# Storing the last four output tiles of an RMSNorm-matmul in smaller pieces

## The chip, the cores and the metric

One core of a Trainium2 chip. The metric is the device time of one execution in microseconds. Times are medians over several runs, and a kernel is compared with the kernel before by runs of the same rounds on the same chip. The profile covers one execution; its span, from first to last instruction, is some 2 us shorter than the time. The runs below used several chips, and the table of profiles mixes them.

## The reference

```python
def setup_inputs():
    batch, seq, dim, out_dim = 16, 1024, 512, 768
    # x: float32 (batch, seq, dim); gamma: ones; weight: float32 (dim, out_dim) * 0.1; eps = 1e-5

def reference(x, gamma, weight, eps):
    rms = np.sqrt(np.mean(x ** 2, axis=-1, keepdims=True) + eps)
    x_norm = x / rms * gamma
    return np.matmul(x_norm, weight).astype(np.float32)
```

That is 16,384 rows. The kernel works on 128 tiles of 128 rows; a tile's output is 128 x 768 float32, 384 KB, 3 KB for each of 128 partitions.

## The kernel before

The kernel casts x to bf16, transposes it on TensorE, multiplies by the weights (gamma folded in), and applies the row's 1/rms when the sums leave PSUM. Outputs gather in groups of eight tiles. A table says after which tile how many tiles are stored at once:

```python
    opening = [1, 2, 1, 2, 2]
    last = NT // OG - 1                       # NT = 128 tiles, OG = 8 tiles in a group
    o_first, o_size = stretches(OG, {0: opening, 1: [4, 4], last - 1: [4, 4], last: [2, 2, 2, 1, 1]})
    ...
    def store(i):
        first, n = o_first[i], o_size[i]
        if i == first + n - 1:
            nc.sync.dma_start(out=rows(out, first, n), in_=held(o_tiles, OG, first, n))
    ...
    def finish_tile(i, acc, engine):
        scale(engine, out_tile(i), acc[:, :O], rstd_of[i])
        store(i)
    ... # the main loop calls finish_tile for all tiles but the last two
        for i in (NT - 2, NT - 1):
            for lo, hi, engine in ((0, WIDE, nc.scalar), (WIDE, O, nc.vector)):   # WIDE = 512, O = 768
                a = accumulator()
                for k in range(K):
                    matmul(i, k, a, lo, hi)
                scale(engine, out_tile(i)[:, lo:hi], a[:, lo:hi], rstd_of[i])
            store(i)
```

Every load of x and every store goes through the sync queue, the queue that the sync engine (SP in the profiles) feeds. Its transfers are spread over 16 DMA engines, each of which moves its share in packets. The last four tiles are called A, B, C and D below (tiles 124 to 127): before, A and B are stored together, C alone, D alone.

Of the kernel before, what the change touches and what calls it, by code (L numbers as in the profile page):

```python
# [18 lines left out]
def kernel(  # L19
# [8 lines left out]
    nc = tc.nc  # L28
# [3 lines left out]
    out = out.flatten_outer_dims()  # L32
# [3 lines left out]
    NT = N // P  # L36
    NP = NT // 2
    XG, OG = 16, 8
# [7 lines left out]
    def stretches(group, parts):  # L46
        first, size, i = {}, {}, 0
        for g in range(NT // group):
            for n in parts.get(g, [group]):
                for t in range(i, i + n):  # L50
                    first[t], size[t] = i, n
                i += n
        return first, size

    opening = [1, 2, 1, 2, 2]
    last = NT // OG - 1
    x_first, x_size = stretches(XG, {0: opening + [4, 4], 1: [4, 4, 8]})
    o_first, o_size = stretches(OG, {0: opening, 1: [4, 4], last - 1: [4, 4], last: [2, 2, 2, 1, 1]})

    def rows(ap, i, n):  # L60
        if i < XG:
            return ap[i * P:(i + n) * P, :].rearrange("(p t) d -> p t d", t=n)
        return ap.rearrange("(g p t) d -> g p t d", p=P, t=XG)[i // XG, :, i % XG:i % XG + n, :]
# [13 lines left out]
    def held(tiles, group, i, n=1):  # L77
        return tiles[i // group][:, i % group:i % group + n, :]
# [8 lines left out]
    def load_until(i):  # L87
        while starts and starts[0] < i:
            load(starts.pop(0))

    def cast(i, engine, n=1):
        if i // 2 not in xb_tiles:
            xb_tiles[i // 2] = xbp.tile([P, 2, D], BF16, name="xb")
        engine.tensor_copy(out=xb_tiles[i // 2][:, i % 2:i % 2 + n, :], in_=held(x_tiles, XG, i, n))  # L94

    def square(i, ssq):
        jk = junk.tile([P, D], BF16, name="jk")
        nc.scalar.activation(out=jk, in_=held(x_tiles, XG, i)[:, 0, :], func=AF.Square, accum_out=ssq)  # L98

    def root(i, n, ssq):  # L100
        rms = stats.tile([P, 4], F32, name="rms")
        nc.scalar.activation(out=rms[:, :n], in_=ssq[:, :n], func=AF.Sqrt, scale=1.0 / D, bias=eps_sb)  # L102
        rstd = stats.tile([P, 4], F32, name="rstd")
        nc.vector.reciprocal(out=rstd[:, :n], in_=rms[:, :n])  # L104
        for t in range(n):
            rstd_of[i + t] = rstd[:, t:t + 1]

    def norms(i, n):
        ssq = stats.tile([P, 4], F32, name="ssq")
        for t in range(n):  # L110
            square(i + t, ssq[:, t:t + 1])
        root(i, n, ssq)
# [18 lines left out]
    def transpose_tile(i):  # L131
        for h in range(2):
            transpose_word(i // 2, i % 2, h)
        evac(i // 2, i % 2, 1)

    def scale(engine, dst, src, r):
        if engine is nc.scalar:
            nc.scalar.mul(out=dst, in_=src, mul=r)  # L138
        else:
            nc.vector.tensor_single_scalar(out=dst, in_=src, scalar=r, op=mybir.AluOpType.mult)  # L140

    def accumulator():
        return opsum.tile([P, 2, WIDE], F32, name="ops").rearrange("p a b -> p (a b)")

    def out_tile(i):
        if i // OG not in o_tiles:
            o_tiles[i // OG] = outp.tile([P, OG, O], F32, name="ot")
        return o_tiles[i // OG][:, i % OG, :]
# [5 lines that stand above are left out]
# [6 lines left out]
    def matmuls(i, acc, ks, feed=None):  # L160
        for k in ks:
            matmul(i, k, acc, 0, WIDE)
            if feed:
                feed()
            matmul(i, k, acc, WIDE, O)
# [4 lines that stand above are left out]
# [16 lines left out]
    with tc.manual_schedule():  # L186
        g_row = singles.tile([2, P, 2], F32)
        nc.scalar.dma_start(out=g_row, in_=gamma.rearrange("(h w c) -> h w c", w=P, c=2))

        wv = weight.rearrange("(h w c) o -> w h (c o)", w=P, c=2)  # L190
        touched = singles.tile([P, 2, 1], F32)
        nc.scalar.dma_start(out=touched, in_=wv[:, :, 0:1])
        nc.scalar.preload_act_table(AF.Sqrt)  # L193
        load_until(3)
        w_f32 = singles.tile([P, K, O], F32)
        for h in range(2):
            nc.sync.dma_start(out=w_f32[:, 2 * h:2 * h + 2, :].rearrange("p c o -> p (c o)"), in_=wv[:, h, :])
        load_until(2 * XG)


        warm = singles.tile([P, WIDE], BF16)
        nc.vector.memset(warm, 0.0)  # L202
        eps_sb = singles.tile([P, 1], F32)
        nc.vector.memset(eps_sb, float(eps))  # L204
        ident_f = singles.tile([P, P], F32)
        make_identity(nc, ident_f)
        spare = accumulator()

        def warm_up(n):
            for _ in range(n):  # L210
                nc.tensor.matmul(out=spare[:, :WIDE], lhsT=warm[:, :P], rhs=warm, start=True, stop=True)  # L211

        w_bf = singles.tile([P, K, O], BF16)

        def weights(k, engine, lo=0, hi=O):
            scale(engine, w_bf[:, k, lo:hi], w_f32[:, k, lo:hi], g_sb[:, k % 2, k // 2:k // 2 + 1])


        ssq = stats.tile([P, 4], F32, name="ssq")
        warm_up(6)  # L220
        cast(0, nc.vector)
        square(0, ssq[:, 0:1])
        gp = tpsum.tile([P, 2, 2], F32, name="tp")
        for c in range(2):
            nc.tensor.transpose(out=gp[:, c, :], in_=g_row[:, :, c], identity=ident_f[:2, :2])  # L225
        g_sb = singles.tile([P, 2, 2], F32)
        nc.vector.tensor_copy(out=g_sb, in_=gp)  # L227
        transpose_tile(0)
        warm_up(3)
        cast(1, nc.vector)  # L230
        cast(2, nc.gpsimd)
        square(1, ssq[:, 1:2])
        square(2, ssq[:, 2:3])
        transpose_tile(1)
        transpose_tile(2)
        warm_up(2)

        acc = [accumulator() for _ in range(4)]
        weights(0, nc.vector, 0, WIDE)
        weights(0, nc.vector, WIDE, O)  # L240
        weights(1, nc.scalar)
        for k in (0, 1):
            for i in range(3):
                matmuls(i, acc[i], [k])
        root(0, 3, ssq)
        weights(2, nc.vector)
        weights(3, nc.scalar)
        cast(3, nc.gpsimd)
        matmuls(0, acc[0], [2, 3])
        finish_tile(0, acc[0], nc.scalar)  # L250
        transpose_tile(3)
        norms(3, 1)
        matmuls(1, acc[1], [2, 3])
        finish_tile(1, acc[1], nc.vector)
        cast(4, nc.gpsimd)
        cast(5, nc.gpsimd)
        matmuls(2, acc[2], [2, 3])
        finish_tile(2, acc[2], nc.scalar)
        matmuls(3, acc[3], [0, 1, 2, 3], feeder([2], [0, 2, 2, 0], alone=True))
        finish_tile(3, acc[3], nc.vector)  # L260
        cast(6, nc.gpsimd, 2)
        cast(8, nc.gpsimd, 2)
        norms(4, 2)


        one, two, both = [1, 1, 0, 1, 1, 0, 0, 0], [1, 0, 1, 0, 1, 0, 1, 0], [1, 1, 1, 1, 1, 1, 1, 1]
        for j in range(2, NP):
            load_until(2 * j + AHEAD)
            if j + 3 < NP:
                cast(2 * j + 6, nc.gpsimd, 2)  # L270
            if j + 1 < NP:
                norms(2 * j + 2, 2)
            if j == NP - 1:
                break
            if j < 4:
                feed = feeder([j + 1], one)
            elif j == 4:
                feed = feeder([5, 6], both)
            elif j + 2 < NP:
                feed = feeder([j + 2], two)  # L280
            else:
                feed = None
            for i, engine in ((2 * j, nc.scalar), (2 * j + 1, nc.vector)):
                a = accumulator()
                matmuls(i, a, range(K), feed)
                finish_tile(i, a, engine)


        for i in (NT - 2, NT - 1):
            for lo, hi, engine in ((0, WIDE, nc.scalar), (WIDE, O, nc.vector)):  # L290
                a = accumulator()
                for k in range(K):
                    matmul(i, k, a, lo, hi)
                scale(engine, out_tile(i)[:, lo:hi], a[:, lo:hi], rstd_of[i])
            store(i)


# [33 lines left out]
```

## Time and profile before

| | before |
|---|---|
| median time | 210.76 us of the first three runs (210.81 with the runs beside the changed kernel) |
| span of the profiled execution | 208.6 us, clock 0.998 |
| PE busy | 95% |
| DMA queue q1, share of 16 engines | 97.0% |
| end of the last scaling | 203.59 us |

The page gives shares over the whole span, then slices of it, then the chain of work that ended last. The last five microseconds show in a table of stretches, which one asks for with chosen limits; after the stretch and its length come the busy times of PE, PEld, DVE, ACT and POOL (TensorE, its weight load, VectorE, ScalarE, GpSimd), and its last columns are the granted clock, the mean busy share of the 16 DMA engines, and GB/s. The prediction shows these lines. A share of 0.06 there is one engine in sixteen. A packet counts in the stretch in which it starts, so a share can come out a little over 1.

### The profile page before, as it was taken

The page shows a single profiled execution, that of the slowest core. Times are in us where ns is not written, and L with a number is a line of the kernel's source. Part 1 is how long each engine was busy: PE and PEld are TensorE (multiplying, and loading weights), DVE is VectorE, ACT ScalarE, POOL GpSimd, SP SyncE. Part 2 cuts the span into 40 slices and gives each one's busy share as a digit, 9 for nine tenths or more (in the row PEclk, how much of TensorE's full clock was granted, in tenths as well). Part 3 has the DMA queues.
Part 4 walks back from the last instruction along what each step waited for, and adds up shares of the span by engine and source line. Part 5 has one row for each costly group of instructions (what it writes and reads, how often), then busy time and mean ns, then how long its engine had stood idle before and what let it go on. Part 6 is the DMA issues. An engine that isn't in the chain of part 4 may idle for free.

```text
span 208.6 us, 3553 instructions
## 1 busy us (share of the span) xinstructions
PE 199.0 (95%) x1268; PEld 137.7 (66%) x1293; DVE 111.6 (54%) x204; ACT 158.2 (76%) x388; POOL 65.8 (32%) x71
## 2 busy tenths in 40 slices
PE   7799999999999999999999999999999999999990
PEld 3366777666766776677667666766776667667650
DVE  2555654654564465456546545654664565456450
ACT  4589787787778778777877877787787778778850
POOL 1058532303631343215323063311533054230000
PEclk9999999999999999999999999999999999999999
DMA  6999999999999999999999999999999999899885
GB/s 216 399 431 415 424 398 433 478 408 394 438 448 421 410 438 434 440 412 424 448 437 432 396 438 438 434 412 432 438 427 456 405 424 437 353 443 386 361 349 225
DMA packets 6630, 85.69 MB, mean 411 GB/s; under 512 B 978, under 2 KB 980, under 8 KB 3156
## 3 DMA queue, kind: packets, MB, share of 16 engines
q1 hardware_dynamic: 6336, 85.46, 97.0%
q8 instruction: 10, 0.16, 0.3%
q10 hardware_dynamic: 276, 0.00, 0.1%
q14 instruction: 8, 0.07, 0.1%
HBM read 35.13 MB, written 50.33 MB: 410 GB/s over the span
## 4 chain that ended last, share of the span: by engine, by line
PE 91%; DMA 3%; DVE 1%; ACT 1%; issue 1%; SPq 0%; DVEq 0%
PE ops L156 78%; PE tp L121 13%; DMA w_f<-in_weight_dram 3%; DVE ot L140 1%; ACT ot L138 0%; SPq L83 0%; ACT jk L98 0%; DVE w_bf L140 0%; DVE xT L128 0%; ACT rms L102 0%; DVE rstd L104 0%; DVEq L140 0%
## 5 line engine op out<-in xcount | busy, mean ns | idle before, releaser
L156 PE MATMUL ops<-w_bf,xT 128*128 128x512 bf16 (+1 forms) x999 | 192.5, 324 | 2.8 <-DVE w_bf L140 1.4
L156 PEld LDWEIGHTS <-xT 128*128 128x128 bf16 x1024 | 100.2, 98 | 57.8 <-issue 1.9
L94 POOL CAST xb<-xt 128x1024 bf16<-128x1024 f32 (+1 forms) x65 | 65.1, 1016 | 120.0 <-PE tp L121 62.2
L128 DVE COPY xT<-tp 128x1024 bf16<-128x1024 bf16 (+1 forms) x67 | 44.5, 667 | 81.0 <-PE tp L121 81.0
L138 ACT ACTIVATE ot<-ops,rstd 128x768 f32<-128x768 f32 (+1 forms) x65 | 58.1, 895 | 37.6 <-PE ops L156 36.8
L98 ACT ACTIVATE jk<-xt 128x512 bf16<-128x512 f32 x128 | 78.7, 619 | 1.1 <-DMA xt<-in_x_dram 1.1
L121 PE MATMUL tp<-ident_f,xb 128*128 128x128 f32 x256 | 69.2, 275 | 0.1
L140 DVE TENSOR_SCALAR ot<-ops,rstd 128x768 f32<-128x768 f32 (+1 forms) x65 | 64.5, 992 | 2.9 <-PE ops L156 2.8
L121 PEld LDWEIGHTS tp<-ident_f,xb 128*128 128x128 f32 x256 | 36.1, 142 | 3.8 <-issue 0.7
L98 ACT ACTIVATION_READ_ACCUMULATOR jk<-xt 128x1 f32 x128 | 24.4, 191 | 0.0
L102 ACT ACTIVATE rms<-ssq,eps_sb 128x2 f32<-128x2 f32 (+1 forms) x64 | 18.9, 296 | 2.0
L104 DVE RECIPROCAL rstd<-rms 128x2 f32<-128x2 f32 (+1 forms) x64 | 10.0, 156 | 3.3 <-ACT rms L102 3.2
L211 PE MATMUL ops<-warm 128*128 128x512 bf16 x11 | 4.8, 585 | 1.2 <-DVE eps_sb L204 1.2
L138 ACT ACTIVATE w_bf<-w_f,g_sb 128x768 bf16<-128x768 f32 x2 | 1.9, 936 | 2.6 <-DMA w_f<-in_weight_dram 2.6
L211 PEld LDWEIGHTS <-warm 128*128 128x128 bf16 x11 | 1.4, 134 | 2.6 <-issue 1.4
L193 ACT ACT_TABLE_LOAD x1 | 1.3, 1283 | 1.8 <-issue 1.8
L94 DVE CAST xb<-xt 128x512 bf16<-128x512 f32 x2 | 1.0, 491 | 2.4 <-DMA xt<-in_x_dram 2.4
L140 DVE TENSOR_SCALAR w_bf<-w_f,g_sb 128x512 bf16<-128x512 f32 (+2 forms) x3 | 1.4, 484 | 1.2 <-DMA w_f<-in_weight_dram 1.2
L225 PEld LDWEIGHTS tp<-ident_f,g_row 2*128 2x128 f32 x2 | 0.3, 201 | 0.8 <-issue 0.8
L202 DVE MEMSET warm<- 128x256 uint32 x1 | 0.3, 272 | 0.9 <-PEq L312 0.9
L225 PE MATMUL tp<-ident_f,g_row 2*128 2x2 f32 x2 | 0.4, 264 | 0.0
L227 DVE COPY g_sb<-tp 128x4 f32<-128x4 f32 x1 | 0.2, 161 | 0.4 <-PE tp L225 0.4
(7 smaller groups left out, 1.0 us busy)
## 6 DMA issues: line engine op xcount, KB each, us to landing
out_dram<-ot SPq DMA_DIRECT2D x12, 3072.0 KB, 15.1
xt<-in_x_dram SPq DMA_DIRECT2D x6, 4096.0 KB, 19.2
out_dram<-ot SPq DMA_DIRECT2D x4, 1536.0 KB, 10.8
out_dram<-ot SPq DMA_DIRECT2D x6, 768.0 KB, 9.6
xt<-in_x_dram SPq DMA_DIRECT2D x4, 1024.0 KB, 13.9
xt<-in_x_dram SPq DMA_DIRECT2D x1, 2048.0 KB, 18.8
xt<-in_x_dram SPq DMA_DIRECT2D x3, 512.0 KB, 6.2
w_f<-in_weight_dram SPq DMA_DIRECT2D x2, 768.0 KB, 7.1
```

The source lines that it names most:

```text
L94: engine.tensor_copy(out=xb_tiles[i // 2][:, i % 2:i % 2 + n, :], in_=held(x_tiles, XG, i, n))
L98: nc.scalar.activation(out=jk, in_=held(x_tiles, XG, i)[:, 0, :], func=AF.Square, accum_out=ssq)
L102: nc.scalar.activation(out=rms[:, :n], in_=ssq[:, :n], func=AF.Sqrt, scale=1.0 / D, bias=eps_sb)
L104: nc.vector.reciprocal(out=rstd[:, :n], in_=rms[:, :n])
L121: nc.tensor.transpose(out=tp_tiles[j][:, t, h, :], in_=words[:, lo:lo + P], identity=ident_f)
L128: nc.vector.tensor_copy(out=dst[:, t:t + n, :], in_=src[:, t:t + n, :])
L138: nc.scalar.mul(out=dst, in_=src, mul=r)
L140: nc.vector.tensor_single_scalar(out=dst, in_=src, scalar=r, op=mybir.AluOpType.mult)
L156: nc.tensor.matmul(out=acc[:, lo:hi], lhsT=xT_tiles[i // 2][:, i % 2, k // 2, :, k % 2], rhs=w_bf[:, k, lo:hi], start=(k == 0), stop=(k == ...
L193: nc.scalar.preload_act_table(AF.Sqrt)
L211: nc.tensor.matmul(out=spare[:, :WIDE], lhsT=warm[:, :P], rhs=warm, start=True, stop=True)
L225: nc.tensor.transpose(out=gp[:, c, :], in_=g_row[:, :, c], identity=ident_f[:2, :2])
```

## The change

Its intent is to start the last stores earlier and to make the very last one small, so that less is left to move after the last scaling.

```diff
-    o_first, o_size = stretches(OG, {..., last: [2, 2, 2, 1, 1]})
+    o_first, o_size = stretches(OG, {..., last: [2, 2, 1, 1, 1, 1]})
@@
                 scale(engine, out_tile(i)[:, lo:hi], a[:, lo:hi], rstd_of[i])
-            store(i)
+                if i == NT - 1:
+                    nc.sync.dma_start(out=rows(out, i, 1)[:, 0, lo:hi], in_=out_tile(i)[:, lo:hi])
+            if i < NT - 1:
+                store(i)
```

(The first two lines are cut; the entries left out are equal.) A and B are stored one by one, and D in two blocks of 512 and 256 columns.

More of the change, by code (lines that the diff above doesn't have):

```diff
@@ L57 @@
     x_first, x_size = stretches(XG, {0: opening + [4, 4], 1: [4, 4, 8]})
-    o_first, o_size = stretches(OG, {0: opening, 1: [4, 4], last - 1: [4, 4], last: [2, 2, 2, 1, 1]})
+    o_first, o_size = stretches(OG, {0: opening, 1: [4, 4], last - 1: [4, 4], last: [2, 2, 1, 1, 1, 1]})
     def rows(ap, i, n):
```

## The prediction

> **What bounds the kernel now.** I read the page first: the busy shares, the slices and the chain that ended last.
>
> ```profile
> PE 199.0 (95%) x1268; PEld 137.7 (66%) x1293; DVE 111.6 (54%) x204; ACT 158.2 (76%) x388; POOL 65.8 (32%) x71
> PEclk9999999999999999999999999999999999999999
> DMA  6999999999999999999999999999999999899885
> ...
> q1 hardware_dynamic: 6336, 85.46, 97.0%
> q8 instruction: 10, 0.16, 0.3%
> ...
> q14 instruction: 8, 0.07, 0.1%
> ...
> PE 91%; DMA 3%; DVE 1%; ACT 1%; issue 1%; SPq 0%; DVEq 0%
> ```
>
> TensorE is the body's bound (91% of the chain, full clock), with the DMA engines hardly less full (97%). The change touches none of the body: the instruction order of PE, DVE, ACT and POOL is the same in both kernels, and only the sync queue gains two issues. So the case is decided in the last microseconds, and I read the timeline of the end next.
>
> ```profile
> 199.17 4.82 SPq L153 DMA_DIRECT2D out_dram<-ot  x4
> 199.20 0.90 ACT L138 ACTIVATE ot<-ops,rstd 128x768 f32<-128x768 f32 x1 [0.37 <-PE ops L156]
> 200.50 1.02 DVE L140 TENSOR_SCALAR ot<-ops,rstd 128x768 f32<-128x768 f32 x1 [1.35 <-PE ops L156]
> 201.37 0.69 ACT L138 ACTIVATE ot<-ops,rstd 128x512 f32<-128x512 f32 x1 [1.26 <-PE ops L156]
> 201.80 0.48 DVE L140 TENSOR_SCALAR ot<-ops,rstd 128x256 f32<-128x256 f32 x1 [0.28 <-PE ops L156]
> 202.67 0.69 ACT L138 ACTIVATE ot<-ops,rstd 128x512 f32<-128x512 f32 x1 [0.61 <-PE ops L156]
> 203.10 0.48 DVE L140 TENSOR_SCALAR ot<-ops,rstd 128x256 f32<-128x256 f32 x1 [0.81 <-PE ops L156]
> ```
>
> Call the last four tiles A, B, C, D. A is scaled by ScalarE until 200.10, B by VectorE until 201.52, C in two blocks until 202.28, D in two blocks until 203.36 (512 columns) and 203.58 (256 columns). Narrow windows of the same view give the stores: the pair before A at 199.17, the pair A+B at 201.60, C at 202.74, D at 203.66. Compute is over at 203.58 and the span at 208.6: 5.0 us of tail. Where they go is in the table of stretches.
>
> ```profile
> 202.00:202.45 0.45, 0.45 (x3) 0.20 (x2) 0.29 (x1) 0.06 (x1) 0.00 (x0) 1.00 0.37 150
> 202.45:204.40 1.95, 0.62 (x5) 0.29 (x3) 0.48 (x1) 0.69 (x1) 0.00 (x0) 1.00 0.98 400
> 204.40:206.40 2.00, 0.00 (x0) 0.00 (x0) 0.00 (x0) 0.00 (x0) 0.00 (x0) 1.00 0.96 382
> 206.40:207.20 0.80, 0.00 (x0) 0.00 (x0) 0.00 (x0) 0.00 (x0) 0.00 (x0) 1.00 0.06 23
> 207.20:208.60 1.40, 0.00 (x0) 0.00 (x0) 0.00 (x0) 0.00 (x0) 0.00 (x0) 0.72 0.00 0
> ```
>
> The last two columns are the DMA engines' mean busy share and GB/s. From 202.45 to 206.40 the engines work off a backlog at 0.96 to 0.98. Before it lies a hole of 0.45 us with a share of 0.37. After it come 0.8 us at 0.06, which is 1/16: one engine alone still has packets. The individual packets say the same: most engines end near 206.42, and then 3 KB packets follow each other about 117 ns apart until 207.18. I call that engine the late one.
>
> Why is it late? The packet lists of two short windows, 193 to 194 and 204.6 to 205.1, show instruction fetches among the data:
>
> ```profile
> q8 instruction: 1, 0.02, 6.3%
> ```
> ```profile
> q14 instruction: 1, 0.01, 3.9%
> ```
>
> The 16 KB fetch of queue 8 starts at 193.45 and takes 1.01 us; a 12 KB data packet beside it takes 1.43 us where the others take 0.46 to 0.50. From there one engine is late. It ends the pair before A at 202.67, when the others ended near 201.98: 0.69 late. It ends A+B at 204.71 (others 204.40): it used the hole to catch up, and was never idle itself. At 204.71, on the heels of that very packet, the 8 KB fetch of queue 14 takes 0.31 us, and that engine's next packets are slower (one takes 294 ns for 121). So it ends 0.75 late.
>
> **What the Trainium skill says.** "DMA: Bandwidth & Descriptors", section "Why a DMA increments its semaphore by 16 and not by 1": a DMA runs on up to 16 engines that finish independently, and only the full count means that all has landed. The trace agrees: of the 16 increments of D's store, 15 are in by 206.87 and the last comes at 207.64. The same page, "Queues, rings and completion order": each engine takes turns between the queue rows that it has work for, by packet; the 1.43 us packet beside the fetch agrees. "Runtime: NRT & Kernel Launch", section "Instruction fetch mechanics": each sequencer fetches its next 16 KiB through DMA; the ten 16 KB fetches of queue 8 are such. The first page's "Anatomy of one DMA" puts most of a fixed cost of some 2 us in the write receipt. Here the last data packet ended at 207.18 and the increment came at 207.64: 0.46 us, less than the page would make one think.
>
> **The change part by part.**
> 1. A is stored alone, so its issue moves from 201.60 (with B) to about 200.18 (A's end 200.10, plus the 0.08 us that lies between B's end and the old issue). An issue reaches the engines 0.85 us later (201.60 to 202.45), so A is ready at 201.03, before the engines end the previous pair at 201.98. The hole of 0.45 us goes, for the 15 engines that have it.
> 2. D in two blocks: the 512 columns issue at 203.36 + 0.08 = 203.44, not 203.66. The 256 columns follow after D's end, 203.66, or after the sync queue is free (0.44 to 0.48 us between back-to-back issues at the start of the kernel): about 203.9. They reach the engines at about 204.75, when there is still over 1 us of backlog. Neither the earlier nor the later one moves the end.
> 3. More packets. Of one store each engine has 8. A 6 KB packet takes 234 ns and a 3 KB packet 121, so a packet costs about 8 ns over its bytes: A+B split is 8 x (2 x 121 - 234) = 64 ns more. For D, 3 KB at 121 becomes 2 KB at 83 (81 to 84 measured for the x loads) and 1 KB at about 46 by the same line: 8 x 8 = 64 ns more. Two more completion writes are 2 x 9 = 18 ns. Sum: +0.15 us per engine.
> 4. The end: the sync engine's records show it passing five semaphore waits in order, and D's completion is in the third of them (207.66); two more at 207.73 and 207.79 and a drain at 207.85 come after it. Completion semaphores go round eight lanes, so the last store moves from the lane of the third wait to that of the fifth. Two waits of 0.063 us no longer lie behind it: -0.13 us.
>
> For 15 engines: -0.45 + 0.15 = -0.30 us. They would end near 206.1. For the late engine: no hole to fill, its bytes and its two fetches are the same, so +0.15 us, at 207.33. The end waits for it. Sum on the path: +0.15 - 0.13 = +0.02 us. The tail keeps its length: 210.76 + 0.02 = 210.78, from which I take a little for the first rival: 210.7.
>
> **The rivals.**
> First, the late engine is less late than the one profile shows. The fetch at 204.71 comes after the last issue, and two more sync instructions could move it or put it on an engine at another moment. Without its 0.31 + 0.17 us the late engine would end at 206.85 and the kernel would gain about 0.45, to 210.3. For it: fetches are not data and nothing fixes their time. Against it: the fetch of queue 8 at 193.45 comes from a long instruction stream that the change leaves alone, and both fetches met the same engine. One in five.
> Second, the drain is not the bound but the last issue's latency: issue to landing is 4.0 us for D. If that were a fixed cost, the later second issue (203.66 to 203.9) would give 211.0. Against it: the share of 0.96 before 206.40 says the 4.0 us are queueing; 0.85 + 0.98 + 0.46 would be 2.3 for a store on idle engines. One in ten.
> Third, 1 KB packets cost as much as 2 KB ones (81 ns): 8 x 35 = 0.28 us more, to 211.0. No 1 KB packets of this queue are in the trace but two. One in ten.
> Fourth, the naive reading: all of the hole is gained, -0.45 us, with the last store's data smaller by two thirds: 210.2. It needs the late engine not to exist.
>
> **Range and chances.** Most weight at 210.6 to 210.9, a tail to 210.3 for the first rival and to 211.0 for the second and third; the three runs of before spread by 0.3 us. Range 210.3 to 211.1. 2% would be 4.2 us, nearly the whole tail of 5.0; no rival reaches a quarter of it. Faster by over 2%: 0.01; within 2%: 0.98; slower: 0.01.
>
> **What would show it.** In the profile of the changed kernel: six issues from the sync queue after 199.1 with the first at about 200.2; a DMA share near 1 at 202.00 to 202.45; the share falling at about 206.1; then a stretch of 0.06 that is longer than before (about 1.2 us for 0.8) and ends near 207.3; an instruction fetch of queue 14 near 204.7. It would be wrong if the stretch of 0.06 were gone or as short as before with an earlier end, if the second block of D issued after 205, or if the body's length moved by more than 0.2 us.

## The result, and the profile after

| | before | after |
|---|---|---|
| median time, us | 210.81 (210.56 to 210.94, 6 runs) | 210.81 (210.24 to 211.32, 6 runs) |
| ratio | | 1.0001, 95% interval 0.9984 to 1.0018 |
| span of the profiled execution, us | 208.6 | 209.5 |

A ratio is the mean time of one kernel's fast runs over that of the other's of the same rounds, so it is not quite the ratio of the medians. The profiled execution of the changed kernel was its slowest run of the six (211.32 us), and that of the kernel before was a quick one (210.38 us), so the two spans must not be read as what the change costs.

The timeline of the changed kernel at its end (start, duration, engine; x gives how many merged; in brackets the idle time before and what ended it):

```profile
199.34 3.52 SPq L153 DMA_DIRECT2D out_dram<-ot  x4
199.37 0.90 ACT L138 ACTIVATE ot<-ops,rstd 128x768 f32<-128x768 f32 x1 [0.37 <-PE ops L156]
...
203.27 0.48 DVE L140 TENSOR_SCALAR ot<-ops,rstd 128x256 f32<-128x256 f32 x1 [0.82 <-PE ops L156]
203.55 0.98 SPq L297 DMA_DIRECT2D out_dram<-ot  x2
```

The body came 0.17 us later than in the first profile of before. Allowing for that, the issues are within 0.1 us of where they were expected: A at 200.30, the first block of D at 203.55, the second at 203.97. The stretches of the changed kernel, moved by the same 0.17 us:

```profile
202.17:202.62 0.45, 0.45 (x3) 0.20 (x2) 0.29 (x1) 0.05 (x1) 0.00 (x0) 1.00 1.03 416
202.62:204.57 1.95, 0.61 (x5) 0.29 (x3) 0.48 (x1) 0.69 (x1) 0.00 (x0) 1.00 1.01 401
204.57:206.20 1.63, 0.00 (x0) 0.00 (x0) 0.00 (x0) 0.00 (x0) 0.00 (x0) 0.98 0.96 364
206.20:207.30 1.10, 0.00 (x0) 0.00 (x0) 0.00 (x0) 0.00 (x0) 0.00 (x0) 0.50 0.19 71
207.30:208.30 1.00, 0.00 (x0) 0.00 (x0) 0.00 (x0) 0.00 (x0) 0.00 (x0) 0.50 0.06 23
```

The hole of before (0.37) is gone: 1.03. The full stretch now ends at about 206.2 instead of 206.4. Then come 1.1 us at 0.19, about three engines, and a further microsecond at 0.06: one engine alone. The packet list of that last microsecond shows little else than pieces of D: 17 packets, of which two are completion writes (under 512 B), eight are of 1 KB and seven of 2 KB:

```profile
DMA packets 17, 0.02 MB, mean 23 GB/s; under 512 B 2, under 2 KB 10, under 8 KB 17
```

What was gained before 206.2 was waited away after it.

### The profile page after: what moved, and what is told of

It reads as the page before. It is cut to its first block, busy times and chain, and to the rows that moved or that the text cites. A ratio compares the mean times of both kernels' runs of the same rounds, so it can differ in the third digit from the quotient of the medians.

```text
span 209.5 us, 3557 instructions
## 1 busy us (share of the span) xinstructions
PE 198.4 (95%) x1268; PEld 137.4 (66%) x1293; DVE 111.7 (53%) x204; ACT 158.2 (76%) x388; POOL 65.6 (31%) x71
## 4 chain that ended last, share of the span: by engine, by line
PE 91%; DMA 3%; DVE 1%; ACT 1%; issue 1%; SPq 0%; DVEq 0%
PE ops L156 78%; PE tp L121 13%; DMA w_f<-in_weight_dram 3%; DVE ot L140 1%; ACT ot L138 0%; SPq L83 0%; ACT jk L98 0%; DVE w_bf L140 0%; DVE xT L128 0%; ACT rms L102 0%; DVE rstd L104 0%; DVEq L140 0%
## 5 line engine op out<-in xcount | busy, mean ns | idle before, releaser
L211 PE MATMUL ops<-warm 128*128 128x512 bf16 x11 | 4.2, 520 | 1.2 <-DVE eps_sb L204 1.2
```

What stands on the lines that cost most here:

```text
L211: nc.tensor.matmul(out=spare[:, :WIDE], lhsT=warm[:, :P], rhs=warm, start=True, stop=True)
```

## The experiments

In the expectations, rival 1 is the prediction's fourth (the hole counts in full, because all engines together set the end) and rival 2 its second (a fixed latency).

The trace records, for every DMA, when each of the 16 engines reported its share as landed (16 increments of a semaphore, the counter that the kernel waits on). From these comes the table that most readings rest on. "Typical" is the median increment of the last store, "last" is the one that the kernel waits for; both in us after the end of the last scaling of the same execution.

```
profile of                  scaling ends   typical     last    last - typical    span
before                          203.59      +3.14     +4.06         0.92        208.6
before, again                   204.05      +3.14     +4.05         0.92        209.1
D split alone                   203.59      +3.20     +4.13         0.93        208.6
D split alone, again            204.20      +3.19     +3.90         0.70        209.0
after                           203.76      +2.77     +4.95         2.17        209.5
after, again                    204.03      +2.75     +3.79         1.04        208.6
A, B split alone                204.68      +2.70     +3.53         0.83        209.1
finer last 24 tiles             203.76      +2.66     +4.63         1.98        209.4
A+B not stored                  203.06      +2.68     +3.31         0.63        207.4
one more load, 8 engines        203.84      +3.39     +4.90         1.51        209.6
one more load, 7 engines        203.80      +3.46     +4.69         1.23        209.4
one more load, 15 engines       204.55      +3.80     +4.46         0.66        209.9
one more load, 16 engines       203.52      +3.76     +5.13         1.38        209.6
```

Two things in these profiles change how the table is to be read.

First, the late engine is not alone. For the pair before A, the first profile of before shows 13 completions within 0.15 us (201.91 to 202.06) and three late ones (202.47, 202.77, 202.82); the other profiles of this table show two to four increments over 0.3 us behind the median. Below, "the late engine" is the latest of these few.

Second, the end of the scaling moves by 1.6 us from profile to profile (203.06 to 204.68), mostly for the same reason. The load of tiles 32 to 47, issued at 28.5 to 29.7 us, has its median increment at 47.8 to 48.7 us but its last at 50.2 to 52.0, and the cast on GpSimd waits for the last one. "After, again" shows it, with TensorE idle behind it:

```profile
51.45 2.02 POOL L94 CAST xb<-xt 128x1024 bf16<-128x1024 f32 x2 [11.27 <-DMA xt<-in_x_dram]
52.54 0.33 PE L121 MATMUL tp<-ident_f,xb 128*128 128x128 f32 x1 [0.75 <-POOL xb L94]
```

In twelve of the fourteen profiles the scaling ends 152.73 us after that last increment, to within 0.01 us (153.36 in the first of before, 153.00 in the first of after). So a late engine also holds up the compute, and a short tail after a late scaling is no gain in time.

**A and B one by one, D whole.** The edit is the diff's first hunk alone.

> The first half of the change alone: A and B stored one by one, D still whole. Theory (one late DMA engine that is never idle sets the end; its bytes are unchanged): no gain; +0.06 us for eight more packets, so within 0.2 us of before, ratio 0.999 to 1.001, while the DMA share at 202.0 to 202.45 rises from 0.37 to over 0.8. Rival 1 (the hole of 0.45 us counts for the end): -0.4 us, ratio 0.998. Rival 2 (issue-to-landing latency of the last store is fixed): no change.

Measured: 210.88 us against 210.72, ratio 1.0000 (0.9985 to 1.0015). In its profile the scaling ends 1.09 us later than in the first of before; the hole's place, moved by that much, reads

```profile
203.09:203.54 0.45, 0.45 (x3) 0.20 (x2) 0.29 (x1) 0.06 (x1) 0.00 (x0) 1.00 1.06 423
```

so the hole is filled, and the typical engine is 0.44 us earlier (+2.70 for +3.14). The last increment too comes 0.53 us sooner after the scaling, but only because this scaling was late: it comes at 208.21, against 207.65 and 208.11 in the two profiles of before. The time does not follow the typical engine: rival 1's 0.998 is outside the interval, if only just.

**D in two blocks, A and B together.** The edit is the diff's second hunk alone.

> The second half of the change alone: D in two column blocks, A+B still together. Theory: late engine +0.06 us of packets, D's completion one lane further, -0.06 us: 210.8, ratio 0.999 to 1.001. Rival 1: the hole at 202.0 to 202.45 stays, so no gain either, +0.06. Rival 2: the second block is issued at about 204.0 rather than 203.66: +0.3 us, ratio 1.0015.

Measured: 210.59 us against 210.86, ratio 0.9986 (0.9962 to 1.0010), too wide to say. It was run once more:

> D in two column blocks alone, once more, because its first ratio of 0.9986 had an interval from 0.9962 to 1.001. Theory: nothing to gain, ratio within 0.001 of 1.000. If splitting D alone were worth 0.3 us, the ratio would again be 0.9986.

Measured: 210.67 us against 210.69, ratio 0.9996 (0.9984 to 1.0008). So the block split alone is worth nothing that these runs can see; in the first rounds the kernel before scattered more widely (210.37 to 212.05), which is a likely reason for the first ratio, not a shown one. No part of the change makes a version that beats both.

**The store of A+B left out.** Wrong on purpose; a fixed part of the output is never written.

```diff
-        if i == first + n - 1:
+        if i == first + n - 1 and i != NT - 3:
```

> Wrong on purpose: the kernel before without the store of the pair A+B, so that every DMA engine has eight 6 KB packets less in the tail. Theory and rival 1 (the end waits for a backlog): 8 x 0.24 = 1.9 us less backlog, of which the latency of D on idle engines (0.85 + 0.98 + 0.46 after the issue at 203.66) leaves about 1.7 us: 209.1, ratio 0.992. Rival 2 (the latency of D's store is a fixed 4.0 us): no change, 210.8.

Measured: 209.46 us against 210.72, ratio 0.9942 (0.9922 to 0.9962): -1.2 us. The end does wait for a backlog; rival 2, a fixed latency of 4.0 us, is out. The run doesn't tell the theory from rival 1, which forecast the same: all 16 engines lost packets. The gain is less than the 1.7 expected. Part of it shows in the trace: D was issued 0.45 us after its scaling instead of 0.07 (the same delay fell on C in the kernel before), and D landed 2.86 us after its issue where I had 2.3. The stores of this profile land in

```profile
out_dram<-ot SPq DMA_DIRECT2D x4, 384.0 KB, 2.9
```

with four such stores counted, two of them at the kernel's beginning. Before, it was 4.0.

**The changed kernel again.**

> The changed kernel once more, for a second profile and five more times. Theory: 210.8, ratio 1.000 within 0.001; single times scatter over 1 us, as the late engine's lateness differs from execution to execution; in the profile the last of D's 16 increments comes 0.7 to 2.5 us after their median. Rival 1: ratio 0.998 and an end set by all the engines together, lateness below 0.5 us.

Measured: 210.81 us against 210.72, ratio 0.9995 (0.9980 to 1.0010), single times from 210.39 to 211.03. The end of this profile reads

```profile
205.00:206.40 1.40, 0.00 (x0) 0.00 (x0) 0.00 (x0) 0.00 (x0) 0.00 (x0) 1.00 0.98 375
206.40:207.50 1.10, 0.00 (x0) 0.00 (x0) 0.00 (x0) 0.00 (x0) 0.00 (x0) 0.95 0.11 40
207.50:208.60 1.10, 0.00 (x0) 0.00 (x0) 0.00 (x0) 0.00 (x0) 0.00 (x0) 0.50 0.00 0
```

with 1.1 us at 0.11, under two engines' worth, instead of two microseconds at three engines and then one: the same program, its latest engine 1.04 us late here and 2.17 us in the first profile. That difference of 1.1 us is as large as the spread of the changed kernel's six times (1.08 us). **The kernel before again** was looked at for the same reason:

> The kernel before once more, for a second profile. Theory: the last of D's 16 increments again comes 0.5 us or more after their median, by an amount that differs from the first profile's 0.92; the 4 us before the end of the compute again show a hole in the mean share of the engines.

Measured: 210.88 us (one run), lateness 0.92 us: the same as in the first, where a different one was expected. The mean share over 202.45 to 204.40 was 0.84, so there was a hole again.

**The last 24 tiles in finer stores.**

```diff
-    o_first, o_size = stretches(OG, {..., last - 1: [4, 4], last: [2, 2, 2, 1, 1]})
+    o_first, o_size = stretches(OG, {..., last - 2: [4, 4], last - 1: [2, 2, 2, 2], last: [2, 2, 1, 1, 1, 1]})
```

> The last 24 tiles stored in smaller parts (4+4, then 2+2+2+2, then 2+2+1+1+1+1), so that more holes between 177 and 203 us are filled. Theory: the late engine has no hole there to fill (it is 1 to 3 us late through the whole stretch), it only gets some 32 more packets of 8 ns overhead each: +0.2 us, 210.8 to 211.2, ratio 1.000 to 1.002. Rival 1 (the mean of the engines counts): the slices after 177 us fall about 3 us short of full, the tail after the last issue at 203.66 would shrink to the latency of D: -1.5 us, 209.3, ratio 0.993. Rival 2: no change.

Measured: 211.24 us against 210.72, ratio 1.0018 (1.0002 to 1.0034), a little slower, as the theory had it; rival 1 had 0.993. Its stretches, then those of before:

```profile
177.00:182.00 5.00, 5.00 (x35) 3.49 (x34) 2.76 (x6) 3.76 (x10) 1.56 (x2) 1.00 0.97 413
192.00:197.00 5.00, 5.00 (x34) 3.48 (x33) 2.94 (x6) 3.76 (x10) 0.00 (x0) 1.00 0.78 318
197.00:200.00 3.00, 3.00 (x20) 1.90 (x19) 1.69 (x3) 2.60 (x7) 0.00 (x0) 1.00 0.73 298
200.00:203.00 3.00, 3.00 (x20) 1.76 (x18) 1.50 (x2) 1.12 (x3) 0.00 (x0) 1.00 0.97 394
```
```profile
177.00:182.00 5.00, 4.95 (x34) 3.46 (x33) 2.59 (x5) 3.76 (x10) 1.40 (x2) 1.00 0.88 378
192.00:197.00 5.00, 4.95 (x35) 3.50 (x34) 2.77 (x6) 3.76 (x10) 0.00 (x0) 1.00 0.82 334
197.00:200.00 3.00, 3.00 (x21) 1.87 (x20) 1.69 (x3) 2.60 (x7) 0.00 (x0) 1.00 0.85 352
200.00:203.00 3.00, 3.00 (x20) 1.65 (x17) 1.50 (x2) 1.12 (x3) 0.00 (x0) 1.00 0.88 363
```

The hole at 177 to 182 was filled (0.88 to 0.97) and came back later, at 192 to 200, presumably because engines that have moved their bytes sooner then wait for the compute. The typical engine ended earlier (+2.66), the late one did not. It was hardly idle there: its increments for the stores issued at 181.10 and 196.67 lie 10.0 us apart (192.70 and 202.72) for five pairs of tiles that take 9.4 (5 x 8 packets of 0.235), while the typical engine's lie 11.1 apart. So here a hole filled in the mean did not lighten the engine that ends last.

**One more load in the tail, on part of the engines.** After the store of the pair before A, 8, 15, 16 or 7 rows of x of 16 KB each are loaded into a tile that nobody reads. The Trainium skill ("DMA: Bandwidth & Descriptors", section "Why a DMA increments its semaphore by 16 and not by 1") states how many of the 16 engines a DMA uses: the largest number up to 16 that divides the outer dimension on both sides, and for this kind of queue the lowest-numbered ones. The trace agrees as to the number: 8, 15, 16 and 7 packets of 16 KB, and as many increments that come as the data land. That they are the lowest-numbered engines no run here shows.

```diff
+    extra = singles.tile([P, 8 * D], F32)
@@
             nc.sync.dma_start(out=rows(out, first, n), in_=held(o_tiles, OG, first, n))
+        if i == NT - 5:
+            nc.sync.dma_start(out=extra[0:8*8:8, :], in_=x[0:8*8, :].rearrange("(p t) d -> p (t d)", t=8))
```

> The kernel before with one more load, issued right after the store of the pair before A: 8 rows of x of 16 KB each, into a tile that nobody reads. It gives 8 of the 16 DMA engines one more packet of about 0.61 us (the 16 KB load's packets at 21 us took that) in the tail. Theory: if the late engine is one of these eight, one of the eight packets starts 0.7 us or more after the others and the end moves by about +0.6 us, ratio 1.003; if not, the eight have slack (0.45 us hole and 0.9 us lateness) and nothing changes, ratio 1.000. Rival 1: half of the engines by 0.61 less the hole of 0.45: under 0.1 us. Rival 2: no change.

> The same with 15 rows, so 15 of the 16 engines get a packet of 16 KB. Theory: +0.6 us if the late engine is among the 15, nothing if it is the sixteenth; the start of the latest packet against the others tells which. Rival 1: 0.61 less the hole of 0.45, +0.15 us, ratio 1.0007. Rival 2: no change.

> The same with 16 rows: every engine gets a packet of 16 KB, the late one too. Theory: +0.6 us in full, as the late engine has no hole, less 0.06 us for one wait fewer at the end: 211.3, ratio 1.0026. Rival 1 (the hole swallows it): +0.15 us, ratio 1.0007. Rival 2: no change.

> The extra load with 7 rows: only the first seven engines get a packet of 16 KB. With 8 rows one of eight packets started 0.8 us after the others. Theory, if the late engine is the eighth: the seven packets start within 0.3 us of one another and the end does not move, ratio 1.000. Theory, if it is one of the first seven: one packet starts 0.5 us or more late and the end moves by +0.6 us, ratio 1.003 as with 8 rows. Rivals 1 and 2: no change either way.

Measured, with the starts of the 16 KB packets:

```
engines   time, us   before, us   ratio (95%)                  packets start at
8         211.48     210.79       1.0049 (1.0020 to 1.0078)    7 in 202.45-202.55, one at 203.33
15        211.43     210.79       1.0028 (1.0013 to 1.0042)    13 in 203.09-203.23, then 203.63, 203.84
16        211.45     210.79       1.0030 (1.0015 to 1.0045)    13 in 202.04-202.26, then 203.08, 203.24, 203.37
7         211.26     210.66       1.0028 (1.0011 to 1.0045)    6 in 202.50-202.58, one at 202.99
```

By the medians each costs 0.60 to 0.69 us, whether 7 or 16 engines get the load. With 7 or 8, at most half of the engines had more to do, and the typical engine ended only 0.25 to 0.32 us later than before, but the last one 0.63 to 0.84 us later. Exactly one of the eight packets starts late, by 0.8 us. The completion writes show that it went to the latest engine of all: that one ended the pair before A at 203.32, two others, outside the eight, at 202.82 and 202.89. With seven, one packet still starts late (by 0.4 us, between the 0.3 and the 0.5 that I had set as limits), but its engine was not the latest: it ended that pair at 202.98, two engines outside the seven at 203.15 and 203.34. The load, done at 203.69, put it behind them. So the added work counts when it falls on one of the late engines; the latest is not shown to be always the same one, and the eighth engine is not singled out. With 16 three packets start late, as many as there were late engines in the profile of before.

The runs with 15 and 16 are weaker evidence than I had thought. Their packets took 0.8 to 0.95 us on most engines instead of 0.61 (so did five of the eight in the run with 8, at 0.78 to 0.86), more than the hole swallows, and the typical engine also ended over 0.6 us later. Rival 1's +0.15 us was worked out for 0.61 and can't be refuted by these two.

**C and D kept off the sixteenth engine.** Their stores were cut into rows 0 to 119 and rows 120 to 127. By the section quoted above these go to 15 and to 8 engines, and 15 and 8 increments come as the data land; that it is the sixteenth that is left out rests on the page.

```diff
-            nc.sync.dma_start(out=rows(out, first, n), in_=held(o_tiles, OG, first, n))
+            for lo, hi in ((0, 120), (120, P)) if i >= NT - 2 else ((0, P),):
+                nc.sync.dma_start(out=rows(out, first, n)[lo:hi], in_=held(o_tiles, OG, first, n)[lo:hi])
```

> The kernel before with the stores of C and D each in two parts, rows 0 to 119 and rows 120 to 127. 120 rows divide over 15 engines, 8 rows over 8, so the sixteenth engine gets no packet of C and D, the first eight get nine of each, the others eight. Theory: the end is the late engine's. If that is the sixteenth, it loses 16 packets (2 us) and the end falls back to the next-latest, 0.5 to 0.8 us sooner: 210.1, ratio 0.996 to 0.998, and the last part's increments close up to within 0.5 us of their median. If it is one of the first eight: 2 more packets, +0.25 us, 211.0; one of the others: 210.8. The parts' increments tell which. Rival 1 (all engines' backlog): half of them have two packets more, +0.25 us in any case. Rival 2: the last issue comes 0.44 us later, +0.4 us.

Measured: 211.29 us against 210.86, ratio 1.0016 (0.9993 to 1.0040). The lateness of D's 120 rows did shrink to 0.38 us, but because the typical engine became slower: 77 of the 256 packets of 3 KB took 171 to 404 ns (median still 121; in the profile of before two of 256 were over 160), and the typical increment of these rows came 4.07 us after the scaling instead of 3.14. D's last 8 rows were issued 1.43 us after the scaling instead of 0.07, and landed at +4.63, so a late issue may have set this end too. The run says nothing of which engine is late, and is no way to relieve one.

## Why the prediction was right, and where not

- **The time** (210.7 forecast, 210.81 measured, ratio 1.0001): right, and for its main reason. The hole is filled and the typical engine gains; the end is set by a late engine, and it does not come sooner. The number alone decides little: the times of three of the four rivals (210.3, 211.0, 211.0) lay inside the range, and the forecast sum of +0.02 us is far below what the interval can resolve (some 0.36 us either way). What supports the mechanism are the profiles and the experiments.
- **Step 1, A's issue and the hole:** right. The share went from 0.37 to 1.03. Only, the hole belonged to 13 engines, not to 15 (see the completions above). The typical engine's gain was forecast as 0.30 us and is 0.37 and 0.39 in the two profiles of after, against both of before.
- **Step 2, the two blocks of D:** right. The issues came at 203.55 and 203.97, both before the backlog was gone, and the split alone gives a ratio of 0.9996.
- **Step 3, packets:** right. 1 KB packets took 45 ns and 2 KB packets 84 in the profile of after, for 46 and 83. The prediction's third rival (81 ns for 1 KB) is out. The trace of before could have told: its two 1 KB packets, which are of another queue (q10), took 44 ns.
- **Step 4, the waits at the end:** right. D's last increment came at 208.70, the fifth wait passed at 208.72 and the drain followed at 208.79; before, the third wait passed at 207.66 and the drain came at 207.85. That is 0.13 us less.
- **The late engine's size and origin:** here a step failed. The prediction wrote of the 16 KB fetch at 193.45: "From there one engine is late". Three readings of the trace were off. The 12 KB packet of 1.43 us did not run beside that fetch: it started at 194.44, as the fetch ended (194.46). The latest engine ended the pair before A at 202.82, not 202.67. And the lateness is older than the fetch: in the same trace the store issued at 187.00 already has its last increment 2.40 us after the median, and the load issued at 3.07 us has 1.2. Lateness is there from the first microseconds, grows to between 3 and 5 us in the body of every profile and shrinks in the holes of the last 15 us; that it is one and the same engine throughout isn't shown. So the predicted stretch of one engine (1.2 us, ending near 207.3) held in neither profile: in one the late engine's last packet ended at 208.27 and it was late by 2.17, in the other by 1.04. Two of the prediction's signs failed as well: the fetch of queue 14 expected near 204.7 came at 204.31 and 203.87, and the end of the body, which was not to move by more than 0.2 us, moved by 0.44 in the second profile of after, but by 0.47 in the second of before too, so that this sign told nothing. The forecast of the time survives because it rests on the late engine's bytes being unchanged and on its never being idle, not on how late it is. For the last 10 us the increments bear this out: in the profile of before, the last increments of the two pairs issued at 196.11 and 199.17 lie 1.93 us apart, about what eight 6 KB packets take (1.88), the medians 2.37. Lateness that differs from execution to execution goes some way to explain the scatter of single times, in both kernels: the one before went from 210.3 to 212.05 over all rounds.
- **What stays open:** what makes an engine late in the first microseconds (lateness at the load issued at about 3.1 us was 0.2 to 1.4 us in different executions), whether the latest engine and the engine that fetches meet are always the same, and why some stores were issued 0.45 us after the scaling they waited for. That a late engine is never idle in the whole body is inferred, not seen: the traces don't name a packet's engine.

## What to carry to other kernels

Before making a tail's stores smaller or earlier, look at what the DMA engines do in the last microseconds one by one, not at their mean share: a stretch of 1/16 at the very end says that one engine sets it, and here filling the holes of the others bought nothing. A gain has to take bytes or packets off that engine, as leaving out a store did (1.2 us, with less for all engines). Look at lateness in the body too: here a load's last increment, 2.1 to 4.1 us after its median, also decided when the compute went on. And when the profiled execution differs from the median by more than the effect in question, profile each kernel twice before reading its end.

## What the Trainium skill lacked or had wrong

- "DMA: Bandwidth & Descriptors", "Why a DMA increments its semaphore by 16 and not by 1", has it that the engines finish independently. It doesn't say by how much in a kernel with a constant queue: in these profiles the last increment of a store came 0.6 to 2.2 us after the median at the end, and up to 5.1 us in the body.
- The same page, "Latency and other measured facts", calls engines 7 and 15 usually slower, with a best guess at the cause that is for the gpsimd queue alone. It says nothing of late engines on the sync queue. Here two to four engines were late, and one packet still started 0.4 us late when the load left the eighth engine out. No run here singles out engine 7.
- The same page, "Anatomy of one DMA", splits the fixed 2 us for the gpsimd queue alone, with most of it in the write receipt. For the sync queue, which this kernel uses, it gives no such split. In the kernel before, 0.85 us lay between the start of the issue and the first packet (0.52 from the issue's end) and 0.46 us between last packet and increment. The section on latency gives about 0.6 us for the first byte.
- "Runtime: NRT & Kernel Launch", "Instruction fetch mechanics", calls the cost of a 16 KiB boundary mostly hidden. It is for the engine that executes; a DMA engine is held for 0.88 to 1.10 us (the ten 16 KB fetches of the kernel before), and a 12 KB packet that started as one ended took 1.43 us instead of 0.46.
- No page that I read warns that packets can slow when stores are cut into 120 and 8 partitions: 77 of 256 packets of 3 KB took 171 to 404 ns in that run, where most of the full stores' took 121.
